# Sixteen key pairs chosen among 80 sums instead of 256, and 80 blocks of activations ahead of the gates in layer 2

## The chip, the cores and the metric

The kernel runs on one core of one Trainium2 chip. The time is device microseconds (us) for one launch, the median of several runs. Beside the runs there is one execution under the hardware profiler; its span and its rows are what the text reads.

## What is computed

Two layers of a hybrid backbone over 256 context tokens and 256 latent tokens with 1024 features. Each layer has a token mixer (attention, a gated delta rule, a linear recurrence) and then a retrieval layer over 16,384 one-neuron experts. The change touches the retrieval layer alone:

```
q = rmsnorm((h @ wq).reshape(ntok, 8, 2, 128))              # 8 heads, 2 halves
s = einsum('nhcd,hckd->nhck', q, subkeys)                   # 128 keys in each half
s_top, i_top = top_k(s, 16)                                 # the 16 best keys of each half
cand = s_top[..., 0, :, None] + s_top[..., 1, None, :]      # 16 x 16 sums of pairs
best, pos = top_k(cand, 16)                                 # the 16 best pairs
idx  = (i_top[..., 0, :, None] * 128 + i_top[..., 1, None, :]) at pos
gate = softmax(best)
act  = gelu(h . u[idx]) * gate;   out = sum over heads and picks of act * v[idx]
```

Layer 1 does this for 512 tokens, layer 2 (the last) for the 256 latent ones only. Since both lists of 16 are sorted, pair (a, b) can be among the 16 best only if (a+1)(b+1) is at most 16.

## The kernel before

**Dense experts.** The kernel doesn't gather rows for most tokens. It computes gelu(h . u) for all 16,384 experts, in 128 blocks of 128 experts, multiplies by a dense gate matrix that is zero where an expert isn't chosen, and multiplies by v. Tokens are columns: N is 384 in layer 1 (the other 128 tokens get their rows by indirect DMA, `fetch`, one row per step on POOL and VectorE) and 256 in layer 2. Each block of u or v (512 KB) is loaded by the SP queue into `wraw` or `vraw` (3 buffers each) and split into a high and a low part: a cast on ScalarE (`wh`, `vh`, L94) and a subtraction on VectorE (`wl`, `vl`, L97). A block of activations is then 8 times three matmuls of N columns (L101 to L103, tile `mm`) and a Gelu on ScalarE (L1006, tile `ge`, 4 buffers).

**Routing.** `queries` computes the scores and the top 16 of each half (`top16`: MAX, MAX_INDEX, MATCH_REPLACE, MAX, MAX_INDEX). `route` then runs `select(g)` for a group of 128 tokens: sums of pairs and `top16` for each of 8 heads, softmax, and for each half a gather of the key's number by comparison with 0..15 (`oh`, `ix`: L1112, L1114, L1116). Layer 1 has four such groups, layer 2 two. After it a loop over passes of 4 tokens builds the gate matrix: VectorE and ScalarE make one-hot rows (`oa`, `ob`), TensorE multiplies them (L1147), ScalarE copies the result to `st` (L1149), and after 32 tokens `st` goes to HBM (2 MB, `gate<-st`). The groups not yet selected are worked off inside this loop.

**Early blocks.** Into both stages `early` puts blocks of activations ahead of the gates: their `ge` is stored to HBM by a DMA on POOL. `REARLY` says how many there are in each layer. One goes with each step of the selects ahead of the loop (20 steps in layer 1, 10 in layer 2), one with every second pass in layer 1 and with every pass in layer 2, and what is left comes after the loop. `experts` afterwards takes the 128 blocks in the order of a list that spreads the late ones (activations not yet computed) among the early ones (activations loaded back, `ge<-early`), multiplies by the gates (`pgt`, loaded for four blocks at a time, L1169 and L1182), splits (`pah`, `pal`) and runs 12 matmuls of 512 columns a block in layer 2.

**What sets the order.** Each engine and the SP queue execute their instructions in one fixed order. A scheduler that builds the program chooses it, from readiness and costs of its own, so that work from different code lines mixes, and an edit changes the order far around it.

Of the kernel before, what the change touches and what calls it, by code (L numbers as in the profile page):

```python
# [13 lines left out]
F32 = mybir.dt.float32  # L14
F32R = mybir.dt.float32r
BF16 = mybir.dt.bfloat16
I32 = mybir.dt.int32
U32 = mybir.dt.uint32
AF = mybir.ActivationFunctionType
ALU = mybir.AluOpType  # L20
# [3 lines left out]
P = 128  # L24
# [15 lines left out]
class Net:  # L40
# [932 lines left out]
    def peer(self, l, T0, x):  # L973
# [3 lines left out]
        gd = self.tc.dram_tile([N // self.TS, P, P, self.TS], F32, name=self.nm("gate"))  # L977
        hd = self.tc.dram_tile([self.REARLY[l], P, N], F32, name=self.nm("early"))
        with self.tc.tile_pool(name=self.nm("gel"), bufs=1, reuse_waits="tile") as gl:
# [16 lines left out]
                next(rows, None)  # L996
            self.rowsdone += 1

    REARLY = (80, 64)
    TS = 32  # L1000

    def expert_h(self, gl, l, j, T0, N):
# [6 lines left out]
    def early(self, gl, l, T0, N, hd, n):  # L1009

        self.wshare = 0.0
        for j in range(self.jearly, min(self.REARLY[l], self.jearly + n)):
            self.nc.gpsimd.dma_start(hd[j], self.expert_h(gl, l, j, T0, N))  # L1013
# [61 lines left out]
    def route(self, rp, l, T0, N, gd, gl, hd, ga, rows, tv, ti, rsN):  # L1075
        nc, V, S, T, I = self.nc, self.V, self.S, self.T, self.I
        mk = lambda shape, tag, dt=F32, bufs=1: self.t(rp, shape, dt, tag, bufs)
        idt, iota = self.C["ident"], self.C["iota"]
        A = NTOK - T0
        NG = A // P  # L1080
        self.jearly = 0
        iT = mk([P, 3, N], "iT")

        def select(g):

            V.tensor_tensor(tv[:, g], tv[:, g], rsN[:, g].unsqueeze(2).to_broadcast([P, 16, 16]), ALU.mult)
            bv, bi = mk([P, 8, 16], "bv"), mk([P, 8, 16], "bi", U32)
            for h in range(8):
                cand, cw = mk([P, 16, 16], "cand", F32, 2), mk([P, 256], "cw", F32, 2)
                V.tensor_tensor(cand, tv[:, g, 2 * h].unsqueeze(2).to_broadcast([P, 16, 16]),  # L1090
                                tv[:, g, 2 * h + 1:2 * h + 2].to_broadcast([P, 16, 16]), ALU.add)
                self.top16(bv[:, h], bi[:, h], cand.rearrange("p a b -> p (a b)"), cw)
                yield
            fetch = g * P >= N
            gt, gs = (ga[1].rearrange("p (a b) -> p a b", b=16) if fetch else mk([P, 8, 16], "gt")), mk([P, 8], "gs")
            V.tensor_tensor(gt, bv, bv[:, :, 0:1].to_broadcast([P, 8, 16]), ALU.subtract)
            S.activation(gt, gt, AF.Exp)
            V.tensor_reduce(gs, gt, AX.X, ALU.add)
            V.reciprocal(gs, gs)
            V.tensor_tensor(gt, gt, gs.unsqueeze(2).to_broadcast([P, 8, 16]), ALU.mult)  # L1100
            tf = mk([P, 16, 16], "tf", BF16)
            V.tensor_copy(tf, ti[:, g])
            sel = []
            for w in range(2):
                pi, pf = mk([P, 8, 16], "pi", U32), mk([P, 8, 16], "pf", BF16)
                if w == 0:
                    V.tensor_scalar(pi, bi, 4, None, ALU.logical_shift_right)
                else:
                    V.tensor_scalar(pi, bi, 15, None, ALU.bitwise_and)
                V.tensor_copy(pf, pi)  # L1110
                oh = mk([P, 8, 16, 16], "oh", BF16, 2)
                V.tensor_tensor(oh.rearrange("p h k v -> p (h k) v"), pf.rearrange("p a b -> p (a b)").unsqueeze(2).to_broadcast([P, P, 16]),  # L1112
                                self.iota16[:, None, :].to_broadcast([P, P, 16]), ALU.is_equal)
                V.tensor_tensor(oh, oh, tf[:, w::2].unsqueeze(2).to_broadcast([P, 8, 16, 16]), ALU.mult)  # L1114
                ix = mk([P, P], "ix", F32, 2)
                V.tensor_reduce(ix, oh.rearrange("p h k v -> p (h k) v"), AX.X, ALU.add)  # L1116
                sel.append(ix)
                yield
            if fetch:
                V.scalar_tensor_tensor(sel[0], sel[1], float(P), sel[0], ALU.mult, ALU.add)  # L1120
                V.tensor_copy(ga[0], sel[0])
                return
            pt = self.px().rearrange("p (a b) -> p a b", a=4)
            for k, src in enumerate((sel[0], sel[1], gt.rearrange("p a b -> p (a b)"))):
                T.transpose(pt[:, k], src, idt)
            S.activation(iT[:, 0, g * P:(g + 1) * P], pt[:, 0], AF.Copy, scale=-1.0)
            S.copy(iT[:, 1:, g * P:(g + 1) * P], pt[:, 1:3])

        for g in ((NG - 1, 0) if ga else (0,)):
            for _ in select(g):  # L1130
                self.early(gl, l, T0, N, hd, 1)
        for n in range(0, N, 4):
            if n % P == 0:
                nxt = select(n // P + 1) if n + P < N else iter(())
            if n % self.TS == 0:
                st = mk([P, P, self.TS], "st", F32, 2)
            pg = (self.px, self.pg, self.acc)[n // 4 % 3]().rearrange("p (a b) -> p a b", a=4)
            a4 = mk([P, 4, P], "oa", F32, 4)
            for k in range(self.OV):
                V.tensor_scalar(a4[:, k], iota, iT[:, 0, n + k:n + k + 1], 0.0, ALU.add, ALU.is_equal)  # L1140
            for k in range(self.OV, 4):
                S.activation(a4[:, k], iota, AF.Abs, bias=iT[:, 0, n + k:n + k + 1])
            S.activation(a4[:, self.OV:], a4[:, self.OV:], AF.Relu, bias=1.0, scale=-1.0)
            for k in range(4):
                b = mk([P, P], "ob", F32, 8)
                ob = V.tensor_scalar(b, iota, iT[:, 1, n + k:n + k + 1], iT[:, 2, n + k:n + k + 1], ALU.is_equal, ALU.mult)  # L1146
                T.matmul(pg[:, k], a4[:, k], b, start=True, stop=True)  # L1147
            m = n % self.TS
            S.copy(st[:, :, m:m + 4].rearrange("p j n -> p n j"), pg)  # L1149
            if m + 4 == self.TS:  # L1150
                nc.scalar.dma_start(gd[n // self.TS], st)
            if n % P % 8 == 0:
                next(nxt, None)
            if n % P == P - 4:
                for _ in nxt:
                    pass
            if n % (self.EV // 2 if T0 else self.EV) == 0:
                self.early(gl, l, T0, N, hd, 1)
            if n % 8:
                self.paced(rows, ob, 1)  # L1160
        self.early(gl, l, T0, N, hd, self.REARLY[l])

# [9 lines left out]
    def expert_terms(self, vp, gl, l, j, T0, N, hd, gt):  # L1172

        nc, I = self.nc, self.I
        mk = lambda shape, tag, dt=F32, bufs=1: self.t(vp, shape, dt, tag, bufs)
        if j < self.REARLY[l]:
            e = self.t(gl, [P, N], F32, "ge", 4)
# [44 lines left out]
    def experts(self, vp, gl, l, T0, N, gd, hd, x, rows):  # L1222

        nc, V, S, T = self.nc, self.V, self.S, self.T
        mk = lambda shape, tag, dt=F32, bufs=1: self.t(vp, shape, dt, tag, bufs)
        E, NT = self.REARLY[l], N // P
        late = [range(j, j + 4) for j in range(E, P, 4)]
# [190 lines left out]
```

## Time and profile before

| | |
|---|---|
| median of 3 runs | 4592.52 us (4588.74 to 4601.06) |
| profiled execution, its own time | 4597.26 us |
| its span | 4595.6 us |
| TensorE busy | 4304.1 us, 94% |
| VectorE busy | 3262.6 us, 71% |
| ScalarE busy | 2345.6 us, 51% |
| granted TensorE clock, mean | 0.96 of full speed |

TensorE is busy nearly all the time, but that is a mean over stages with different limits, and a busy TensorE isn't one at its peak: matmuls overlap, and their ends are modelled. The retrieval layer's routing runs from about 1457 to 1903 us in layer 1 and from 3750 to 4058 us in layer 2; the layer 2 experts follow to 4580 us.

### The profile page before, as it was taken

What the parts mean: (1) busy time and instruction counts of PE and PEld (TensorE: products, weight loads), DVE (VectorE), ACT (ScalarE), POOL (GpSimd) and SP (SyncE); (2) the same over time, 40 slices, a digit from 0 to 9 for tenths busy, and PEclk for the clock granted to TensorE, in tenths of its full rate; (3) what the DMA queues carried; (4) which work ended last, traced back from release to release, by engine and by line L of the source; (5) the groups of instructions that cost most, each with busy time, mean ns of one, the idle gap of its engine ahead of it and who ended that gap; (6) DMA issues with size and microseconds to landing.
All of it is one profiled execution on the core that took longest, in us unless ns stands there. A gap on an engine that the chain in (4) does not pass through costs nothing.

```text
span 4595.6 us, 66921 instructions
## 1 busy us (share of the span) xinstructions
PE 4304.1 (94%) x24379; PEld 3623.5 (79%) x24379; DVE 3262.6 (71%) x7406; ACT 2345.6 (51%) x4145; POOL 453.6 (10%) x428
## 2 busy tenths in 40 slices
PE   6999999999889989999999989989998789989999
PEld 3686877787667889988888856878777689978888
DVE  4767576764469998677888767777675599656665
ACT  4455555553244578533333355656554347844444
POOL 0000000000000222343344300000000001100000
PEclk8999999999999999999999989999998899989999
DMA  4313232225532677899999734223222635676765
GB/s 150 117 60 108 70 106 78 90 72 184 195 106 90 228 253 270 315 335 341 334 334 333 267 119 140 81 83 103 65 83 87 224 131 204 235 238 229 240 231 175
DMA packets 361530, 816.48 MB, mean 178 GB/s; under 512 B 66672, under 2 KB 184944, under 8 KB 357872
## 3 DMA queue, kind: packets, MB, share of 16 engines
q1 hardware_dynamic: 313264, 611.90, 40.3%
q0 software_dynamic: 45056, 158.36, 9.5%
q10 hardware_dynamic: 2880, 41.94, 2.3%
q8 instruction: 191, 3.13, 0.3%
q14 instruction: 139, 1.14, 0.1%
HBM read 713.52 MB, written 98.57 MB: 177 GB/s over the span
## 4 chain that ended last, share of the span: by engine, by line
PE 79%; DVE 11%; DMA 4%; ACT 4%; issue 1%; SPq 0%; ACTq 0%; DVEq 0%
PE mm L103 11%; PE mm L101 11%; PE mm L102 11%; PE acx L101 4%; PE acx L102 4%; PE acx L103 4%; PE px L101 3%; PE px L102 3%; PE px L103 3%; DVE wl L97 2%; DVE ob L1146 1%; PE acg L101 1%; PE acg L103 1%; PE px L872 1%; PE acg L102 1%; DMA wraw<-in_wada 1%
## 5 line engine op out<-in xcount | busy, mean ns | idle before, releaser
L101 PE MATMUL mm<-hh,wh 128*128 128x256 f32 (+2 forms) x2784 | 919.9, 330 | 59.2 <-ACT ge L1006 26.7
L103 PE MATMUL mm<-hh,wl 128*128 128x256 f32 (+2 forms) x2784 | 913.1, 328 | 27.5 <-DVE wl L97 27.1
L102 PE MATMUL mm<-hl,wh 128*128 128x256 f32 (+2 forms) x2784 | 907.7, 326 | 0.0
L94 ACT CAST wh<-wraw 128x1024 fp32r<-128x1024 f32 (+2 forms) x473 | 487.8, 1033 | 697.3 <-PE mm L102 557.2
L97 DVE TENSOR_TENSOR wl<-wraw,wh 128x1024 fp32r<-128x1024 f32 (+2 forms) x473 | 566.2, 1198 | 236.9 <-ACT wh L94 234.8
L101 PEld LDWEIGHTS mm<-hh,wh 128*128 128x128 f32 x2784 | 536.8, 193 | 91.7 <-ACT ge L1006 29.5
L103 PEld LDWEIGHTS mm<-hh,wl 128*128 128x128 f32 x2784 | 535.9, 193 | 59.1 <-DVE wl L97 39.8
L102 PEld LDWEIGHTS mm<-hl,wh 128*128 128x128 f32 x2784 | 536.8, 193 | 23.7 <-issue 2.5
L97 DVE TENSOR_TENSOR vl<-vraw,vh 128x1024 fp32r<-128x1024 f32 x256 | 312.7, 1222 | 148.9 <-ACT vh L94 146.3
L94 ACT CAST vh<-vraw 128x1024 fp32r<-128x1024 f32 x256 | 268.9, 1051 | 280.1 <-PE pg L103 162.6
L94 ACT CAST pah<-ge 128x384 fp32r<-128x384 f32 (+1 forms) x256 | 114.8, 459 | 230.1 <-DVE ge L1182 187.9
L1146 DVE TENSOR_SCALAR ob<-cst,iT 128x128 f32<-128x128 f32 x640 | 183.0, 345 | 55.3 <-PE pg L1147 22.5
L1204 POOL DMA_INDIRECT grow<-in_v,gix x128 | 186.2, 1455 | 252.7 <-DVE gacc L1219 225.8
L1013 POOL DMA_DIRECT2D early<-ge x144 | 80.3, 557 | 1311.7 <-ACT ge L1006 930.9
L101 PE MATMUL mm<-hh,whx 128*128 128x512 f32 (+1 forms) x544 | 203.6, 374 | 2.9 <-ACT tx L800 1.8
L103 PE MATMUL mm<-hh,wlx 128*128 128x512 f32 (+1 forms) x544 | 201.5, 370 | 2.1 <-DVE wlx L97 2.1
L102 PE MATMUL mm<-hl,whx 128*128 128x512 f32 (+1 forms) x544 | 201.8, 371 | 0.0
L101 PE MATMUL px<-vh,pah 128*128 128x512 f32 x512 | 199.5, 390 | 0.0
L102 PE MATMUL px<-vl,pah 128*128 128x512 f32 x512 | 199.3, 389 | 0.0
L103 PE MATMUL px<-vh,pal 128*128 128x512 f32 x512 | 199.1, 389 | 0.0
L1204 POOL DMA_INDIRECT grow<-in_ur,gix x128 | 160.4, 1253 | 303.2 <-DVE gdot L1210 217.5
L1219 DVE SCALAR_TENSOR_TENSOR gacc<-grow,gdot,gacc 128x1024 f32<-128x1024 f32 x127 | 163.1, 1284 | 1.5
(509 smaller groups left out, 10083.3 us busy)
## 6 DMA issues: line engine op xcount, KB each, us to landing
wraw<-in_u SPq DMA_DIRECT2D x256, 512.0 KB
vraw<-in_v SPq DMA_DIRECT2D x256, 512.0 KB
wraw<-in_win SPq DMA_DIRECT2D x192, 512.0 KB
wraw<-in_wada SPq DMA_DIRECT2D x96, 512.0 KB
gate<-st ACTq DMA_DIRECT2D x20, 2048.0 KB
wraw<-in_wbr SPq DMA_DIRECT2D x48, 512.0 KB
pgt<-gate SPq DMA_DIRECT2D x32, 768.0 KB
wraw<-in_wq SPq DMA_DIRECT2D x32, 512.0 KB
```

Of the source, the lines that this page charges most:

```text
L94: self.S.copy(h, src)
L97: return self.V.tensor_tensor(l, src, h.bitcast(F32), ALU.subtract)
L101: mm(out, lh, rh, start=first, stop=False)
L102: mm(out, lh, rl, start=False, stop=False)
L103: mm(out, ll, rh, start=False, stop=last)
L872: T.matmul(sc, a[s, q0:q0 + P], b[s, :nk], start=t == 0, stop=t == 2)
L1013: self.nc.gpsimd.dma_start(hd[j], self.expert_h(gl, l, j, T0, N))
L1146: ob = V.tensor_scalar(b, iota, iT[:, 1, n + k:n + k + 1], iT[:, 2, n + k:n + k + 1], ALU.is_equal, ALU.mult)
L1204: nc.gpsimd.indirect_dma_start(r, None, table, bass.IndirectOffsetOnAxis(ap=ix[:, k:k + 1], axis=0))
L1219: V.scalar_tensor_tensor(acc, r, dot[:, k:k + 1], acc, ALU.mult, ALU.add)
```

## The change

The 256 sums of a head are replaced by 80: a = 0 with all 16 b, a = 1 to 7 with b = 0 to 7, and a = 8 to 15 with b = 0. They are made for all 8 heads at once, by three additions. The search runs over 80 columns. Six small operations on 128 columns turn a place among the 80 into the pair (a, b). And `REARLY` of layer 2 goes from 64 to 80, which layer 1 had already.

```diff
-    REARLY = (80, 64)
+    REARLY = (80, 80)
...
             bv, bi = mk([P, 8, 16], "bv"), mk([P, 8, 16], "bi", U32)
+            cand = mk([P, 8, 80], "cand")
+            s1, s2 = tv[:, g, 0::2], tv[:, g, 1::2]
+            V.tensor_tensor(cand[:, :, :16], s1[:, :, 0:1].to_broadcast([P, 8, 16]), s2, ALU.add)
+            V.tensor_tensor(cand[:, :, 16:72].rearrange("p h (a b) -> p h a b", b=8), s1[:, :, 1:8].unsqueeze(3).to_broadcast([P, 8, 7, 8]),
+                            s2[:, :, :8].unsqueeze(2).to_broadcast([P, 8, 7, 8]), ALU.add)
+            V.tensor_tensor(cand[:, :, 72:], s1[:, :, 8:], s2[:, :, 0:1].to_broadcast([P, 8, 8]), ALU.add)
             for h in range(8):
-                cand, cw = mk([P, 16, 16], "cand", F32, 2), mk([P, 256], "cw", F32, 2)
-                V.tensor_tensor(cand, tv[:, g, 2 * h].unsqueeze(2).to_broadcast([P, 16, 16]),
-                                tv[:, g, 2 * h + 1:2 * h + 2].to_broadcast([P, 16, 16]), ALU.add)
-                self.top16(bv[:, h], bi[:, h], cand.rearrange("p a b -> p (a b)"), cw)
+                self.top16(bv[:, h], bi[:, h], cand[:, h], mk([P, 80], "cw", F32, 2))
                 yield
...
-            for w in range(2):
-                pi, pf = mk([P, 8, 16], "pi", U32), mk([P, 8, 16], "pf", BF16)
-                if w == 0:
-                    V.tensor_scalar(pi, bi, 4, None, ALU.logical_shift_right)
-                else:
-                    V.tensor_scalar(pi, bi, 15, None, ALU.bitwise_and)
-                V.tensor_copy(pf, pi)
+            c8 = lambda tag, dt=BF16: mk([P, 8, 16], tag, dt)
+            hi, lo = c8("phi"), c8("plo")
+            for dst, op, n in ((hi, ALU.logical_shift_right, 3), (lo, ALU.bitwise_and, 7)):
+                pi = mk([P, 8, 16], "pi", U32, 2)
+                V.tensor_scalar(pi, bi, n, None, op)
+                V.tensor_copy(dst, pi)
+            pa, pb, t = c8("pa"), c8("pb"), c8("pt")
+            V.scalar_tensor_tensor(t, hi, 9.0, lo, ALU.is_equal, ALU.mult)
+            V.tensor_scalar(pa, hi, -1.0, 0.0, ALU.add, ALU.max)
+            V.tensor_tensor(pa, pa, t, ALU.add)
+            V.tensor_tensor(lo, lo, t, ALU.subtract)
+            V.tensor_scalar(pb, hi, 1.0, 8.0, ALU.is_equal, ALU.mult)
+            V.tensor_tensor(pb, pb, lo, ALU.add)
+            for w, pf in enumerate((pa, pb)):
```

Three places show how the change moves instructions. The first is VectorE at the start of layer 2's select, right after the scores have been scaled (`tv`); `cand` holds the sums, `bv` and `bi` the chosen values and places, `cw` the working copy. Before:

```order
L1086 TENSOR_TENSOR tv_32942<-tv_32942,rny_33887 128x256 x2
L1090 TENSOR_TENSOR cand_33908<-tv_32942 128x256
L1090 TENSOR_TENSOR cand_33950<-tv_32942 128x256
L1019 MAX bv_33906<-cand_33908 128x8
L1019 MAX bv_33906<-cand_33950 128x8
L1020 MAX_INDEX bi_33907<-bv_33906,cand_33908 128x8
L1021 MATCH_REPLACE cw_33909<-bv_33906,cand_33908 128x256
```

The same place in the changed kernel:

```order
L1090 TENSOR_TENSOR tv_32930<-tv_32930,rny_33875 128x256 x2
L1094 TENSOR_TENSOR cand_33896<-tv_32930 128x8x16
L1095 TENSOR_TENSOR cand_33896<-tv_32930 128x8x56
L1097 TENSOR_TENSOR cand_33896<-tv_32930 128x8x8
L97 TENSOR_TENSOR wl_34070<-wraw_34067,wh_34069 128x1024
L1019 MAX bv_33894<-cand_33896 128x8 x2
L1020 MAX_INDEX bi_33895<-bv_33894,cand_33896 128x8
L1021 MATCH_REPLACE cw_33900<-bv_33894,cand_33896 128x80
```

Three additions stand where each head had one, the searches read 80 columns a head, and a split of a block of u (`wl`) now stands ahead of the first search.

The second place is TensorE at the end of layer 2's gate loop: L1147 (before) and L1161 (changed) are the gate matmuls, `mm` a block of activations, `pah` the experts' own product. Before:

```order
L1147 MATMUL px_37556<-ob_37569,oa_37557 128x128
L1147 MATMUL px_37556<-ob_37572,oa_37557 128x128
L101 MATMUL mm_37790<-hh_32886,wh_37793 128x256
L102 MATMUL mm_37790<-hl_32887,wh_37793 128x256
L103 MATMUL mm_37790<-hh_32886,wl_37794 128x256
L101 MATMUL mm_37790<-hh_32886,wh_37793 128x256
L101 MATMUL acg_37582<-vh_37597,pah_37591 128x512
```

And in the changed kernel, where the block that begins here is followed by six whole blocks and nine matmuls of another before the first `pah`:

```order
L1161 MATMUL px_37844<-ob_37857,oa_37845 128x128
L1161 MATMUL px_37844<-ob_37860,oa_37845 128x128
L101 MATMUL mm_37865<-hh_32874,wh_37868 128x256
L102 MATMUL mm_37865<-hl_32875,wh_37868 128x256
L103 MATMUL mm_37865<-hh_32874,wl_37869 128x256
L101 MATMUL mm_37865<-hh_32874,wh_37868 128x256
```

Four matmuls of a block stood between the last gate matmul and the experts before; now it is 177. The third place is the SP queue around the first load of gates in layer 2. Before, the loads of u and of the first four stored blocks stand ahead of it:

```order
L1178 DMA ge_37651<-early_32930 128x256
L121 DMA wraw_38007<-in_u 128x1024
L121 DMA wraw_38063<-in_u 128x1024
L121 DMA wraw_38119<-in_u 128x1024
L1169 DMA pgt_37586<-gate_32929 128x8x128
L1186 DMA vraw_37595<-in_v 128x1024
```

In the changed kernel two early blocks' loads of u, and all loads of stored blocks, stand behind it:

```order
L121 DMA wraw_38002<-in_u 128x1024
L1183 DMA pgt_38112<-gate_32917 128x8x128
L121 DMA wraw_38036<-in_u 128x1024
L121 DMA wraw_38070<-in_u 128x1024
L1200 DMA vraw_38121<-in_v 128x1024
L1200 DMA vraw_38134<-in_v 128x1024
L1200 DMA vraw_38159<-in_v 128x1024
L1183 DMA pgt_38202<-gate_32917 128x8x128
L1200 DMA vraw_38184<-in_v 128x1024
L121 DMA wraw_38205<-in_u 128x1024
L1200 DMA vraw_38242<-in_v 128x1024
L1192 DMA ge_38114<-early_32918 128x256
```

Of the 80 loads of u for early blocks, 78 are now ahead of the first load of gates and two behind it.

## Rows read from the trace of the kernel before

**Rows 1.** Busy time by stage: window, its length, each engine's busy us (instructions), clock, DMA.

```profile
1457.00:1549.00 92.00, 84.12 (x467) 81.69 (x466) 90.18 (x229) 36.67 (x55) 16.62 (x25) 0.96 0.52 184
1549.00:1741.00 192.00, 171.33 (x1060) 162.65 (x1061) 191.58 (x560) 143.43 (x278) 42.52 (x53) 0.96 0.69 235
1741.00:1869.00 128.00, 126.91 (x850) 126.33 (x850) 110.14 (x312) 107.22 (x206) 35.12 (x43) 1.00 0.85 292
1869.00:1903.00 34.00, 32.11 (x176) 31.38 (x175) 17.43 (x18) 14.96 (x21) 7.97 (x10) 0.95 0.96 353
3750.00:3793.00 43.00, 29.68 (x191) 27.78 (x190) 42.49 (x111) 14.24 (x22) 4.90 (x9) 0.80 0.36 124
3793.00:3868.00 75.00, 70.29 (x561) 68.11 (x561) 73.80 (x212) 60.75 (x115) 9.29 (x17) 0.98 0.60 207
3868.00:4014.00 146.00, 140.64 (x1165) 138.77 (x1165) 99.39 (x261) 118.68 (x227) 19.43 (x36) 0.99 0.64 224
4014.00:4035.00 21.00, 17.53 (x132) 15.88 (x130) 12.65 (x46) 15.80 (x31) 0.54 (x1) 0.95 0.50 183
4035.00:4058.00 23.00, 5.41 (x17) 4.37 (x18) 9.03 (x15) 6.70 (x12) 0.00 (x0) 0.52 0.79 279
4090.00:4580.00 490.00, 490.00 (x2807) 429.74 (x2806) 294.38 (x403) 236.61 (x347) 0.00 (x0) 1.00 0.68 225
```

**Rows 2.** Timeline, TensorE in layer 1's loop, two passes apart: start, length, instruction.

```profile
1802.47 1.05 PE L1147 MATMUL pg<-ob,oa 128*128 128x128 f32 x8
...
1808.42 1.05 PE L1147 MATMUL px<-ob,oa 128*128 128x128 f32 x8
```

**Rows 3.** Timeline, TensorE in layer 2's loop, one pass apart.

```profile
3990.02 1.05 PE L1147 MATMUL px<-ob,oa 128*128 128x128 f32 x8
...
3993.78 1.05 PE L1147 MATMUL pg<-ob,oa 128*128 128x128 f32 x8
3994.67 1.06 PE L1147 MATMUL acx<-ob,oa 128*128 128x128 f32 x8
```

**Rows 4.** Waits, 3750 to 3793: engine, line, waited for: us, times, longest.

```profile
PE mm L103 <- DVE wl L97: 9.7, 3, 7.6
```

**Rows 5.** Waits of TensorE, 1549 to 1741.

```profile
PE mm L103 <- DVE wl L97: 7.0, 10, 1.5
```

**Rows 6.** Timeline of VectorE, 3745 to 3787: searches over 128 and 256 columns, a cast.

```profile
3745.06 0.27 DVE L1022 MAX8 tv<-tw 128x8 f32<-128x128 f32 x1
3745.25 0.07 DVE L1021 MATCH_VALUE_LOAD tw<-tv,sc 128x8 f32 x1
...
3755.34 0.41 DVE L1022 MAX8 bv<-cw 128x8 f32<-128x256 f32 x1
3755.67 0.07 DVE L1021 MATCH_VALUE_LOAD cw<-bv,cand 128x8 f32 x1
...
3785.22 0.22 DVE L1110 CAST pf<-pi 128x128 bf16<-128x128 uint32 x1
```

**Rows 7.** The chain that ended last, 4033 to 4060: start, us, what.

```profile
4033.74 1.24 PE px L1147 x4
4036.09 9.44 DMA gate<-st
4046.02 4.98 DMA vraw<-in_v
4052.59 0.58 PE mm L101
...
4054.75 0.43 PE px L101
...
4059.75 0.23 PE px L102
```

**Rows 8.** Waits of the SP queue, 4000 to 4060.

```profile
SPq L1169 <- DMA gate<-st: 6.9, 1, 6.9
```

**Rows 9.** The chain that ended last, 1884 to 1893, in layer 1.

```profile
1884.07 8.84 DMA vraw<-in_v
```

## The prediction

> **What bounds the kernel now.** I read the busy time by stage first, then the timeline for the price of a pass, then the waits, and last the chain around the end of layer 2's gate loop. In the stages the reader is to see which engine is full [rows 1]. Layer 1's routing has VectorE busy 90.18 of 92 us before the gate loop and 191.58 of 192 us in its first part; there TensorE is busy 171.33 us, at a granted clock of 0.96. From 1741 us on it is the other way round: TensorE 126.91 of 128. Layer 2 repeats this in small: VectorE 42.49 of 43 us before the loop, with TensorE at 29.68 and a clock of 0.80, and 73.80 of 75 while the second select is worked off. From 3868 us TensorE is nearly full, and in the experts entirely (490 of 490). Between them, from 4035 to 4058, TensorE is busy 5.41 of 23 us.
>
> The waits say what TensorE lacks where VectorE is full: the low part of a block of u, which stands in VectorE's queue behind searches. One such wait in layer 2's first select is 7.6 us long [rows 4]; in layer 1's loop ten add up to 7.0 us [rows 5].
>
> The hole at 4035 is the way of the gates through HBM. The last gate matmul ends at 4034.98, the last 2 MB are written from 4036.09 for 9.44 us, a first load behind it lands 4.98 us after 4046.02, and TensorE goes on at 4052.59 [rows 7]. The SP queue waits 6.9 us in this for the write [rows 8]. After it the 512-column matmuls run 0.43 us apart, later 0.23 [rows 7]: the lower of the two clock levels, after TensorE had stood idle.
>
> **The searches.** One search over 128 columns takes 0.19 us of VectorE from start to start, one over 256 columns 0.33, and the load ahead of a replacement 0.06 to 0.07 [rows 6]. That is 0.0011 us a column, so 80 columns cost 0.14. A head had one addition and five searches over 256 columns and three loads: 6 x 0.33 + 0.2 = 2.18 us. It now has five searches over 80: 5 x 0.14 + 0.2 = 0.90. Eight heads save 10.2 us. The three additions cover 128, 448 and 64 columns a partition: 0.19 + 0.54 + 0.12 = 0.85 us. The six new small operations are priced by the 128-column cast, whose length is 0.22 us [rows 6]: 1.3. The shifts and casts of places stay, and so do the gathers. A select saves 8 us. The lower bound takes each search to wait for the end of the one before it: 128 columns last 0.27 us [rows 6], 80 then 0.22, a head costs 1.3, and a select saves 4.9. The order speaks for the upper end: it interleaves two heads, as before.
>
> There are six selects, 48 us of VectorE; the question is how much of it TensorE can use. In layer 1 a block and two passes take 5.95 us when TensorE is the limit [rows 2], so the loop's 48 such pairs need 286 us of the 320 between 1549 and 1869: 34 us of slack. A pass alone takes 0.89, a layer 2 pass with its block 3.76 [rows 3], so a block costs 2.87 us in layer 2 and 5.95 - 1.78 = 4.17 in layer 1. Ahead of the loop 20 blocks need 83 of 92 us. Four selects free 32 us of VectorE against 43 of slack. I take 24 of 32: the gathers remain as bursts in which a pass must wait for VectorE whatever the searches cost. Bounds are 12, where the shorter prices meet those bursts, and 32.
>
> Layer 2's first select is wholly VectorE's: 8 us (5 to 9), as its ten blocks need 28.7 of 43. In the second, 561 matmuls are 17.5 passes with a block, 66 of 75 us [rows 1, 3]: I take 5 of the 8 freed (2 to 8). The selects together give 37 us (19 to 49).
>
> **The 16 blocks.** They leave the experts, where TensorE is full, so 16 x 2.87 = 46 us go from there [rows 1, 3]. They come back on TensorE earlier; the gain is what they find idle. Ten go into the last ten passes. Those took 21 us, from 4014 to 4035, in which 132 matmuls ran: 80 of passes and 52 of blocks that the scheduler had drawn ahead, 8.9 + 6.2 = 15.1 us of need, so 6 us lost. In the stage before, 1165 matmuls are 36.4 passes with a block, 137 us of 146: 0.25 lost a pass [rows 1, 3]. Ten such passes lose 2.5. Gain 3.
>
> In the hole 7.4 blocks now follow the last pass, 21 us of work. The idle time was 17.6 us (4052.59 - 4034.98), and some 12 matmuls at 0.43 in place of 0.23 made it 2.5 longer [rows 7]: 20. Not all goes away. Two of the loads of u stand behind the load of gates in SP's order, and that waits for the write, which lands 10.5 us after the last pass. Five blocks cover 14.4 us. The sixth's load, by the nearest row some 5 us [rows 7], lands at 15.5, and the cast ahead of its first matmul makes it 16.5 to 17: 2.5 us idle. The stored blocks' loads stand behind five loads of v, of which the fourth waits for a free buffer, that is for the first one's cast and subtraction. I put them out at 19.5 and their landing, multiplication and split at 25, when the blocks have ended near 23: 2 more. The clock falls in such pauses: another 2.5. So 7 us stay, and 13 are gained. Edits with one answer: the stores and loads of 16 x 128 KB are hidden by TensorE's work, at a DMA share of 0.68 in the experts [rows 1]; without that cover they are 4 MB, or 19 us at that stage's 225 GB/s. Gain of this part 16 us, with bounds 3 and 23.
>
> The Trainium skill (Trainium Kernel Development and Optimization, Key Constraints) says that transfers issued from SP, ACT and POOL share the same 16 DMA engines and interleave. By it the early blocks' loads lengthen the gate write; six of them are 3.1 MB, and if all of that ran ahead of the chain at the 279 GB/s of that stage, the hole would keep 11 us more and this part would give 5 in place of 16.
>
> Against that stands layer 1, which already has blocks in this place: from 1869 to 1903 TensorE is busy 32.11 of 34 us at a clock of 0.95, with the DMA engines at 0.96 [rows 1], though one load there takes 8.84 us [rows 9]. I keep 16.
>
> **Sum.** 37 + 16 = 53 us off the profiled execution's 4597.3: 4544. That execution is 4.7 us above the median shown, so 4540.
>
> **The rivals.** First, *the hole stays*: loads bunch up behind the gates, each as slow as layer 1's 8.84 us [rows 9]. The sixth block then starts near 23, the stored blocks are ready near 37, and the idle time is 16 us with some 4 of low clock: all that was there. Only the 3 us of the passes remain, 40 in all: 4552. For it speaks the order on SP, against it layer 1's full TensorE.
>
> Second, *the searches save less*: chained searches at 0.22 us, and passes that wait for gathers. The selects give 19, in all 35: 4557. For it speaks that only part of layer 1's idle time lies at the searches. Third, *all is used*: 49 + 23 us: 4520. VectorE's full stages speak for it, the bursts against. Fourth, *both fail*, the searches giving 10 us and the blocks 3: 4579.
>
> The other side: *slower, by the SP queue*. The load of gates waits for the write, and two loads of u and everything later wait behind it. Five blocks cover 14.4 us from the last pass; each us that the write lands later is then a us of idle TensorE. It landed after 10.5 us. To use up 53 us it would have to land some 60 us after the last pass; at 75 it gives 4607. Nothing in the rows comes near: the chain's longest transfer is 9.44 us.
>
> **How the numbers follow.** Forecast 0.55, the hole stays 0.15, searches save less 0.15, all is used 0.09, both fail 0.04, slower 0.02. The low end of the range is the upper bounds' sum of 72 us, 4520, a little widened; the high end the lower bounds, 19 + 3 = 22 us, 4570. No change within measurement is 0.3%, 14 us. Only both failing together comes there, so faster has 0.94.
>
> **What would show it.** Searches over 80 columns 0.14 us apart, and VectorE's busy time about 48 us lower; the loop of layer 1 near 300 us instead of 320; layer 2's stretch before the loop near 35 instead of 43; an idle TensorE of about 5 us, not 17.6, behind the last pass; the experts 46 us shorter. Wrong it would be if layer 1's loop kept its length, since TensorE's waits would then not have been the searches', or if the hole only moved behind the sixth block.

## The result, and the profile of the changed kernel

The changed kernel takes 4542.93 us (median of 4 runs, 4536.66 to 4545.33), the kernel before beside it 4596.39 (4 runs, 4588.74 to 4601.06). The ratio is 0.9883, with a 95% interval of 0.9864 to 0.9902: 53 us less, where 4540 us and a sum of 53 were forecast. The total hides errors in its terms: the searches gave more than forecast, the 16 blocks less.

The profiled execution took 4536.66 us, its span is 4535.0. The page's line of busy times:

```profile
PE 4283.0 (94%) x24379; PEld 3612.7 (80%) x24379; DVE 3214.4 (71%) x7412; ACT 2348.0 (52%) x4145; POOL 457.7 (10%) x444
```

VectorE is 48.2 us less busy than before (3262.6), which is the forecast's figure. The busy time by stage of the changed kernel (the columns of [rows 1]):

```profile
1441.00:1533.00 92.00, 87.33 (x503) 84.52 (x501) 91.63 (x322) 39.59 (x59) 17.63 (x26) 1.00 0.54 185
1533.00:1830.00 297.00, 288.35 (x1911) 285.42 (x1911) 273.77 (x809) 251.00 (x483) 77.66 (x95) 1.00 0.81 278
1533.00:1600.00 67.00, 62.43 (x408) 60.65 (x409) 65.67 (x212) 56.84 (x111) 17.07 (x21) 1.00 0.77 256
1600.00:1650.00 50.00, 46.08 (x301) 45.12 (x300) 49.93 (x162) 40.83 (x79) 12.84 (x16) 1.00 0.78 263
...
3707.00:3748.00 41.00, 34.21 (x249) 31.59 (x250) 40.17 (x136) 19.62 (x34) 5.54 (x10) 0.96 0.46 145
3748.00:3830.00 82.00, 77.91 (x628) 75.81 (x627) 75.22 (x241) 66.54 (x129) 9.86 (x18) 0.98 0.61 205
...
4002.00:4034.00 32.00, 24.55 (x182) 22.81 (x182) 14.22 (x14) 14.87 (x22) 4.34 (x8) 0.95 0.87 309
4034.00:4526.00 492.00, 491.49 (x2678) 425.07 (x2678) 299.78 (x425) 237.73 (x346) 0.00 (x0) 1.00 0.72 234
```

Layer 1's gate loop lasts 297 us instead of 320, and VectorE is full only in its first 117 us, before in the first 192. Layer 2's first select is still VectorE's (40.17 of 41). From the end of the scores to the first gate matmul it lasts 41.1 us; before it was 51.8, of which the window of [rows 1] leaves out the first 7. The whole of it before:

```profile
3743.00:3795.00 52.00, 37.84 (x252) 35.38 (x252) 50.82 (x146) 20.76 (x37) 5.50 (x10) 0.83 0.36 119
```

VectorE does 10.65 us less work in this stretch and the stretch is 10.7 us shorter; TensorE's clock in it rose from 0.83 to 0.96. Between the last pass and the experts 177 matmuls run where there were 4. The experts last 492 us instead of 534, 42 us less and not the 46 of the forecast: 341 matmuls have left them, 14.2 blocks and not 16, since parts of two had been drawn ahead of them before.

VectorE's timeline in that select: searches start 0.15 us apart and the load ahead of one takes 0.05 to 0.06 (0.14 and 0.06 to 0.07 were forecast; [rows 6] has 0.33 for 256 columns):

```profile
3720.10 0.23 DVE L1022 MAX8 bv<-cw 128x8 f32<-128x80 f32 x1
3720.25 0.07 DVE L1021 MATCH_VALUE_LOAD cw<-bv,cand 128x8 f32 x1
3720.30 0.23 DVE L1021 MATCH_REPLACE8 cw<-bv,cand 128x80 f32<-128x80 f32 x1
3720.45 0.08 DVE L1023 MATCH_VALUE_LOAD bi<-bv,cw 128x8 f32 x1
```

Of TensorE's waits in layer 1's loop, those for the low part of u fell to 2.1 us in three waits (before, from 1549 to 1741 alone, [rows 5]):

```profile
PE mm L103 <- DVE wl L97: 2.1, 3, 1.1
```

The table holds, for each stretch, what TensorE lost in it: its length (between the matmuls that bound it) less its matmuls at the steps that the traces show at full clock (0.11 us for 128 columns, 0.12 for 256, 0.17 for 384, 0.23 for 512; rounded here, and the third place moves a row by some 7 us at most, but the differences between these four kernels by less than 0.5). The last two kernels are the first two experiments below.

| lost, us | before | changed | searches alone | blocks alone |
|---|---|---|---|---|
| layer 1, select and loop | 51.4 | 22.4 | 23.7 | 51.5 |
| layer 2, first select | 22.4 | 11.8 | 11.8 | 22.3 |
| layer 2, loop | 24.5 | 18.7 | 21.1 | 20.1 |
| last pass to first `pah` (the hole) | 18.5 | 10.8 | 18.2 | 10.4 |
| experts of layer 2 | 8.2 | 7.2 | 7.8 | 9.9 |
| sum | 125.0 | 70.9 | 82.6 | 114.2 |

The sums differ from before by 54.1, 42.4 and 10.8 us; the medians by 53, 39 and 9.

The chain around the hole, which answers to [rows 7]:

```profile
4004.04 8.69 DMA gate<-st
4012.75 0.38 SPq L1183
...
4014.61 7.52 DMA vraw<-in_v
...
4023.24 1.24 DVE vl L97
4024.49 3.47 DMA vraw<-in_v
...
4030.31 1.05 ACT wh L94
...
4031.38 1.24 DVE wl L97
...
4034.53 0.43 PE acg L101
```

The last gate matmul ends at 4002.64. The gates can be loaded 10.1 us later (4012.75), a first load of v lands 7.52 us after its issue, and a fourth goes out only at 4024.49, when the first one's buffer is free. The first product of the experts comes 32 us behind the last pass. Behind the early blocks TensorE pauses 3.15 us (4028.25 to 4031.40, from start to start), until `wh` of the block that follows is ready; six shorter pauses of 0.48 to 1.68 us lie ahead of it, one of 0.88 behind. The `pah` matmuls begin 0.43 us apart again, eight of them.

The first two of these pauses, 1.68 us at 4008 and 0.72 at 4010, don't come from the loads. TensorE waits there for two casts (`wh`) whose loads had landed at 4000.09 and 4003.84 by the DMA semaphores in the trace. The casts stand behind the second block's Gelu in ScalarE's order:

```profile
4008.43 0.39 ACT L1006 ACTIVATE ge<-mm 128x256 f32<-128x256 f32 x1 [2.49 <-PE mm L103]
4008.71 1.98 ACT L94 CAST wh<-wraw 128x1024 fp32r<-128x1024 f32 x2
```

Every kernel here with 80 or more blocks in layer 2 has both pauses; they are 2.2 of the 10.8 us in the table.

SP's waits around the hole, which answer to [rows 8]:

```profile
SPq L1200 <- DVE vl L97: 11.5, 4, 6.0
SPq L1183 <- DMA gate<-st: 8.4, 1, 8.4
```

### The profile page after: what moved, and what is told of

Read it like the earlier page. It is cut to its first block, busy times and chain, and to the rows that moved or that the text cites. A ratio compares the mean times of both kernels' runs of the same rounds, so it can differ in the third digit from the quotient of the medians.

```text
span 4535.0 us, 67054 instructions
## 1 busy us (share of the span) xinstructions
PE 4283.0 (94%) x24379; PEld 3612.7 (80%) x24379; DVE 3214.4 (71%) x7412; ACT 2348.0 (52%) x4145; POOL 457.7 (10%) x444
## 4 chain that ended last, share of the span: by engine, by line
PE 81%; DVE 10%; ACT 4%; DMA 4%; issue 1%; SPq 0%; ACTq 0%; DVEq 0%
PE mm L103 11%; PE mm L101 11%; PE mm L102 11%; PE acx L101 4%; PE acx L102 4%; PE acx L103 4%; PE px L101 3%; PE px L102 3%; PE px L103 3%; DVE wl L97 2%; PE acg L103 1%; PE acg L101 1%; PE px L872 1%; PE acg L102 1%; PE pg L102 1%; PE pg L101 1%
```

## The experiments

Each time is a median beside the kernel before on the same chip. Three questions were open. Do the two parts add up, and which term is off? What share of the freed VectorE time does TensorE use? And what keeps the hole from closing? For the last one the theories were SP's waits (the gates' write, later the loads of v), casts of v in the way on ScalarE, and the DMA engines themselves.

**The searches alone.** The changed kernel with 64 early blocks:

```diff
-    REARLY = (80, 80)
+    REARLY = (80, 64)
```

> The 80 sums alone, with 64 blocks ahead in layer 2 as before. Theory A (the searches free VectorE where TensorE waits for it): about 40 us less than before, near 4556, ratio 0.991, with layer 1's gate loop near 297 us from its first to its last matmul and layer 2's stretch between the scores and the loop near 41. Theory B (most of the gain comes with the 16 blocks and the new order, not with the searches): at most the 11 us of layer 2's first select, near 4585.

Measured: 4555.25 us (4547.22 to 4557.23), ratio 0.9913 (0.9900 to 0.9927): 39 us less than before, where the forecast's terms add to 37 and theory A had 4556. The table shows 27.7 in layer 1, 10.6 in the first select of layer 2 and 3.4 in its loop.

**The blocks alone.** The kernel before with 80 early blocks:

```diff
-    REARLY = (80, 64)
+    REARLY = (80, 80)
```

> The 16 blocks alone, with 256 sums as before. Theory A: about 12 us less than before, near 4584, ratio 0.997, since the last ten passes and the hole behind them are filled in the same way. Theory B: 40 us or more less. Theory C (the hole only moves behind the sixth block and the scheduler's two late blocks did the rest already): within 3 us of before.

Measured: 4585.48 (4576.52 to 4590.49), 0.9979 (0.9970 to 0.9988), 9 us less; theory A had 4584. The two parts add up: 39 + 9 = 48 by medians and 42.4 + 10.8 = 53.2 by the table, against 53 and 54.1 for both. The term of the blocks is the one that was too large.

**Gates loaded through POOL.** If the remaining hole is SP waiting for the gates' write, with loads of u and v behind it, a load that waits on POOL sets them free:

```diff
-        self.nc.sync.dma_start(gt, gd[:, :, j:j + 4].rearrange("c i j n -> i c j n"))
+        (self.nc.gpsimd if self.T0 else self.nc.sync).dma_start(gt, gd[:, :, j:j + 4].rearrange("c i j n -> i c j n"))
```

> The changed kernel with layer 2's loads of gates issued by POOL instead of SP. Theory A (what is left of the hole is SP standing 8.4 us at the first load of gates, with two loads of u and all of v behind it): the 11 us that TensorE still loses there fall to 3 or 4, near 4536, and the sixth block no longer waits. Theory D (the loads share the DMA engines, and these are the limit there): no change, near 4543.

Measured: 4547.20 (4542.62 to 4554.84), 0.9903 (0.9888 to 0.9918): no gain. The hole is 33.0 us long, the experts lose 11.3. The chain of this run shows why:

```profile
4010.49 9.77 DMA vraw<-in_v
...
4022.62 9.92 DMA vraw<-in_v
```

A load of v now goes out 0.3 us behind the write of the gates instead of 10.6, and takes 9.77 us instead of 7.52; the next one takes 9.92. Much of what SP waited for before is now waited for in the transfers. The gain of theory A is not there. The edit did not set SP free, though: the two loads of u go out at 4017.15 and 4018.29, because SP now waits for `wl`, that is for a free buffer. What SP's wait is worth is left to the five buffers below.

**72, 96 and 112 blocks.** The changed kernel with `REARLY` of layer 2 at 72, 96 and 112.

> The changed kernel with 72 blocks ahead in layer 2: eight more than before, all of them inside the passes, none behind the last one. Theory A (the passes give 4 us, the blocks behind the last pass the rest): the hole loses 18 us again, and the three stretches from the loop to the end of the experts are 785 us long (792.7 before, 788.5 with the searches alone, 778.2 changed), in all near 4551. Theory F (it is the count of stored blocks that helps, wherever they run): half of the gain, near 4548, with the hole half as long.

> The changed kernel with 96 blocks ahead in layer 2. Theory A: 22 blocks, 63 us of TensorE, stand behind the last pass, longer than the 32 us until the first product of the experts, so only the wait of the sixth block, some 4 us, stays of the 11: near 4537. Theory D: more stores and loads in the same stretch cost what they cover, 4543 or more.

> The changed kernel with 112 blocks ahead in layer 2. Theory A: as with 96, since the chain behind the last pass is covered already: 4535 to 4538, the three stretches within 3 us of the 770.4 of 96. Theory D (stores and loads cost DMA time): more than 3 us longer than with 96.

The stretches are those of layer 2 from the first gate matmul to the experts' end, by length; the 64 are the searches alone.

| early blocks | median, us | ratio (interval) | stretches, us | hole and experts, lost |
|---|---|---|---|---|
| 64 | 4555.25 | 0.9913 (0.9900 to 0.9927) | 788.5 | 18.2 + 7.8 |
| 72 | 4550.18 | 0.9896 (0.9881 to 0.9912) | 782.2 | 11.9 + 9.5 |
| 80 | 4542.93 | 0.9883 (0.9864 to 0.9902) | 778.2 | 10.8 + 7.2 |
| 96 | 4536.43 | 0.9872 (0.9857 to 0.9887) | 770.4 | 7.8 + 3.9 |
| 112 | 4539.87 | 0.9878 (0.9863 to 0.9894) | 769.0 | 9.2 + 1.1 |

The rows come from several chips; by the difference from the kernel before on the same chip they are 39, 49, 53, 58 and 60 us less. The 72 don't separate their two theories (4551 and 4548 expected). The stretch of 782.2 us is 3 below what theory A had, and the hole loses 11.9 us and not 18, because the edit did not do what A took it to do: two whole blocks stand behind its last pass, not none. The 112 come out 2 to 5 us above what was expected of them, on a chip where the kernel before took 5 us longer than beside the 96; by the difference they are where they were expected. The first 16 blocks give 10 us of stretch, the next 16 eight (13 and 3 in the series below), the last 16 nothing that can be told from no change. With 96 the work outlasts the loads: the clock stays at 1.00 through the 32 us behind the last pass, in which TensorE is busy 27.98 us (24.55 in the changed kernel). A row of that kernel by window (the last gate matmul is at 4009; run again, see below):

```profile
4009.00:4041.00 32.00, 27.98 (x222) 26.72 (x220) 14.86 (x13) 16.12 (x23) 4.86 (x9) 1.00 0.88 326
```

**Fewer splits of v in the way.** In the chain `wh` of the block that follows stands right behind a cast and a subtraction of v. With two split buffers instead of four in layer 2 the third and fourth cast of v move behind that `wh`:

```diff
-    VB = (4, 4)
+    VB = (4, 2)
```

> The changed kernel with two buffers in place of four for the split blocks of v in layer 2, so that on ScalarE the cast of the first late block of u stands behind two casts of v and not four. Theory E (what is left of the hole is this cast, which waits for v's fourth load): the first product of the experts comes 4 us earlier behind the last pass (28 in place of 32), near 4539, if the experts don't lose by having fewer buffers. Theory D (the rate of the loads): no change there.

Measured: 4555.86 (4546.84 to 4563.22), 0.9908 (0.9895 to 0.9922), 44 us less than before where the changed kernel has 53. The casts were not the cause: the third and fourth no longer stand ahead of `wh`, and its load of u landed at 4029.80, 16.8 us after the load of gates went out, in the changed kernel 17.5. So at most 0.7 us was theirs. `wh` starts 17.56 us after the load of gates in both (4030.53 - 4012.97, in the changed kernel 4030.31 - 4012.75), but that is chance: in this run it stands behind the Gelu of the block before (4030.26), whose matmuls ran 0.21 us apart instead of 0.12.

```profile
4012.97 0.38 SPq L1183
...
4025.79 4.46 issue
...
4030.53 1.04 ACT wh L94
```

What the edit costs lies in the experts, where the stretch grew from 492 to 503 us because TensorE now waits for splits (waits of TensorE from 4034 to 4537):

```profile
PE acg L102 <- DVE vl L97: 7.0, 8, 2.0
```

**Searches over 176 columns.** The sums padded to 176 columns, so that about half of what the searches save is taken back:

```diff
-            cand = mk([P, 8, 80], "cand")
+            cand = mk([P, 8, 176], "cand")
+            V.memset(cand[:, :, 80:], -3.0e38)
...
-                self.top16(bv[:, h], bi[:, h], cand[:, h], mk([P, 80], "cw", F32, 2))
+                self.top16(bv[:, h], bi[:, h], cand[:, h], mk([P, 176], "cw", F32, 2))
```

> The changed kernel with each head's 80 sums padded to 176 columns by a constant that is never chosen: each search costs 0.10 us more, a select 4.0, and one fill of some 0.9. Theory A (VectorE's time in the searches is what TensorE waits for): layer 1's stretch from the scores to the loop's end gets 15 to 20 us longer, layer 2's first select 5, the second 1 or 2: 4563 to 4570. Theory B (it was the new order, not the searches' time): 5 us or less.

Measured: 4565.02 (4559.84 to 4573.78), 0.9933 (0.9919 to 0.9946), 34 us less than before where the changed kernel has 53. Searches start 0.25 us apart:

```profile
3741.48 0.32 DVE L1022 MAX8 bv<-cw 128x8 f32<-128x176 f32 x1
3741.73 0.32 DVE L1019 MAX8 bv<-cand 128x8 f32<-128x176 f32 x1
3741.97 0.07 DVE L1023 MATCH_VALUE_LOAD bi<-bv,cw 128x8 f32 x1
```

This is within what theory A had (4563 to 4570). VectorE's busy time is 3239.8 us, 22.8 below before instead of 48.2: 3.8 us a select instead of 8.0. Layer 1 lost 39.3 us instead of 51.4: 12.1 gained where its four selects freed 15.2, a share of 0.8. In the changed kernel it is 29.0 of 32, 0.9. The forecast had 0.75. Layer 2's first select is 6.3 us longer than in the changed kernel (5 expected), the second not longer (1 or 2 expected). VectorE is full in the first one again (45.23 of 47; the clock is 0.89):

```profile
3727.00:3774.00 47.00, 35.61 (x248) 33.55 (x247) 45.23 (x138) 19.08 (x32) 5.47 (x10) 0.89 0.40 128
```

**Five raw buffers of v; 96 blocks again; both.** In the changed kernel the load of u for the block behind the pause went out at 4024.86, behind the fourth load of v, and landed at 4030.23, just ahead of its `wh` (by the DMA semaphores in the trace). With five raw buffers in layer 2 that load of v waits for nothing; the order on TensorE and ScalarE is the same:

```diff
-        raw = mk([P, 1024], "vraw", F32, 3)
+        raw = mk([P, 1024], "vraw", F32, (3, 5)[l])
...
-            y = mk([P, 1024], "vraw", F32, 3)
+            y = mk([P, 1024], "vraw", F32, (3, 5)[l])
```

It ran together with the changed kernel as it is, the 96 blocks, and 96 blocks with five buffers.

> The changed kernel as it is, beside the three others of this series. It should come out near 4543 us again, 53 us below the kernel before; the three stretches from the scores of layer 2 to the first product behind the last pass and the experts add up to 778 us, as in the first profile of it, and the stretches that no edit touches differ from that profile by up to some 10 us.

> 96 blocks ahead of the gates in layer 2, beside the changed kernel on the same chip. If the 8 us by which its layer 2 stretches were shorter (770.4 against 778.2) are real, its median is 5 to 10 us below that of the changed kernel. If they are scatter, the two medians agree within 3 us.

> The changed kernel with five raw buffers of v in layer 2 instead of three; the order on TensorE and ScalarE stays as it is, and on SP the fourth load of v moves ahead of the load of gates and waits for nothing. Theory G, that the end of the hole is SP's wait: the load of u for the block that begins the experts was issued 22.5 us after the last gate matmul only because the fourth load of v ahead of it waited for the first one's subtraction (11.5 us of waits on SP). Without that wait it goes out 8 us earlier, the pause of 3.15 us ahead of that block is gone, the first product of the experts comes 2 to 4 us earlier, and the stretch from the last pass to it falls from 32 to 28 to 30 us. Theory H, that it is the DMA engines, which are nearly full behind the gates: the same bytes land as late as before, whatever order they go out in, the first product comes within 1 us of where it was, and the time is that of the changed kernel. In the experts themselves, where TensorE is full, both expect nothing.

> Both together: five raw buffers of v and 96 blocks. With 96 blocks there is work left on TensorE long after the loads behind the gates have landed, so neither theory expects the buffers to add anything: the time of the 96 blocks alone, within 3 us. If the two gains added up, it would be 2 to 4 us below it.

| | median, us | runs | ratio (interval) | stretches, us |
|---|---|---|---|---|
| changed, again | 4545.54 | 4542.34 to 4555.79 | 0.9887 (0.9869 to 0.9905) | 775.5 |
| 96 blocks, again | 4538.98 | 4530.08 to 4555.13 | 0.9876 (0.9856 to 0.9896) | 772.7 |
| five buffers | 4542.72 | 4529.92 to 4543.25 | 0.9870 (0.9852 to 0.9888) | 774.7 |
| five buffers and 96 | 4531.11 | 4521.75 to 4543.60 | 0.9852 (0.9831 to 0.9872) | 772.6 |

With five buffers SP's waits for `vl` shrink from 11.5 us to one of 1.0 (waits of SP, 3998 to 4045):

```profile
SPq L1183 <- DMA gate<-st: 9.1, 1, 9.1
...
SPq L1200 <- DVE vl L97: 1.0, 1, 1.0
```

The load of u goes out 4.8 us after the load of gates instead of 12.1, and lands 15.9 us after it instead of 17.5: seven us earlier out, 1.6 earlier in. The hole is 30.4 us long, against 32.0 and 30.9 in the two profiles of the changed kernel. So theory G, SP's wait, is worth at most 1.6 us, and theory H, the DMA engines, holds for the rest but for the 2.2 us of ScalarE's order. The windows of the changed kernel behind the write of the gates show it (the last three columns are the clock, the DMA share and GB/s):

```profile
4013.00:4017.00 4.00, 4.00 (x36) 4.00 (x35) 1.22 (x1) 1.33 (x2) 0.54 (x1) 1.00 0.70 228
4017.00:4030.00 13.00, 9.27 (x69) 8.25 (x67) 6.80 (x6) 7.10 (x10) 2.02 (x4) 1.00 1.01 349
4030.00:4034.00 4.00, 2.13 (x8) 1.84 (x9) 2.61 (x5) 1.78 (x3) 0.15 (x1) 0.62 0.75 254
```

and the same with five buffers:

```profile
4019.00:4031.00 12.00, 9.62 (x64) 9.01 (x62) 6.99 (x6) 7.13 (x11) 1.62 (x3) 0.86 1.04 396
```

The DMA engines are full from the landing of the gates (4016.77) until that load of u is in (4030.23). What they move at that share is not one rate: 349 GB/s here, 396 with five buffers. Nine loads of 512 KB stand in between in either order (two of gates, three of u, four of v).

The 96 blocks are 6.5 and 6.6 us below the changed kernel by the medians of both series (4.3 in the first by the differences from the kernel before), and 5 us by the stretches (771.6 against 776.9, means of two); single runs overlap, so the gain is likely but not shown. The lowest median is that of both edits, 8 us below the 96 blocks, where nothing or 2 to 4 us was expected. But its stretches equal those of the 96 blocks alone, so nothing in the stretches that the buffers touch accounts for the 8 us; whether they are real stays open.

## Why the prediction was right, and where its terms were off

**Searches, layer 1: 24 forecast, 29 measured** (27.7 with the searches alone). The mechanism was right: the searches over 80 columns start 0.15 us apart, VectorE lost 48 us of work, and the waits for `wl` fell. That it was the searches' time and not the new order is shown by the 176 columns, which give back what they cost. The share of the freed time that TensorE would use was set too low, 0.75 in place of 0.9. The bursts of gathers, for which a quarter was set aside, cost little.

**Searches, layer 2: 8 and 5 forecast, 10.6 and 3.4 measured.** In the first select TensorE gained more than the 8.0 us that a select gives. VectorE's rows show why: it is full in that stretch before and after, and its work in it fell by 10.65 us. Before, 72 instructions of the searches stood there, more than the 64 of one select, because a first head of the second select was searched in it; in the changed kernel there are 64. So the new order moved some 2 us of VectorE's work into the second select, where less was then used than forecast. With 176 columns VectorE does 5.6 us less there and 4.3 are gained. TensorE's clock rose as well (0.83 before, 0.89 with 176 columns, 0.96 with 80), but a full VectorE sets the length of the stretch, so no gain is shown to be the clock's. The sum, 14, is near the 13 forecast.

**The blocks in the passes: 3 forecast, 4.4 measured with the blocks alone, 2.4 on top of the searches.** The size is right within what two profiles can tell.

**The hole: 13 forecast, 8.1 measured with the blocks alone, 7.4 on top of the searches.** (With the blocks alone 1.7 were lost again in the experts, in the changed kernel nothing.) This is the term that was mis-sized; the blocks' part is 11 instead of 16. The step that failed is the one in which the stored blocks' loads were put "out at 19.5" and ready "at 25", so that 7 us would stay, where the table has 10.8. The sixth block's load, "by the nearest row some 5 us", was nearly right: it took 5.71 us and landed 16.3 us after the last pass, where 15.5 was forecast. Behind it the loads bunch up, because the early blocks and the experts ask for nine loads, 4.7 MB, within 17.5 us. A first load of v takes 7.52 us, and those behind it land 1.1 to 2.3 us apart. The 4.98 us of [rows 7] was a load with one load of gates ahead of it. The first stored block's load went out 24.6 us after the last pass and landed at 29.5, the load of u for the block that leads the experts landed at 27.6, and the first product came at 31.7. The fourth load of v did wait for a free buffer, as the text said, but an early end of that wait moves the landing by 1.6 us only. The forecast also left out the 2.2 us that ScalarE's order takes behind the second block.

The rival by which the blocks' transfers and the gates' write share the DMA engines had 5 us for this part, the forecast 16; the runs give 9 by medians and 11 by the table, between the two. It did not come in the form in which it was priced: the write of the gates was not lengthened (8.69 us, before 9.44); it was the loads behind it that waited for one another, at a DMA share of 1.01. A stored block of 128 KB from POOL's queue took 2.0 us before the write (3999.52 to 4001.52) and 6.4 us among SP's loads (4015.51 to 4021.95). The Trainium skill (Trainium Kernel Development and Optimization, Key Constraints) says that transfers of the SP, ACT and POOL queues run on the same DMA engines and interleave. These two times agree with it. Layer 1, which was brought against the rule, showed only that TensorE had work enough there; its DMA share of 0.96 [rows 1] was the warning.

**The rivals.** *The hole stays* was nearer the truth than its chance of 0.15 says: its picture of bunched loads is what happened, at less than half its price. *The searches save less* is excluded by the searches alone (39 us, it had 19). *All is used* had 49 us for the searches; they gave 39 by medians and 42 by the table, nearer to the 37 of the forecast, and the blocks stayed far below its 23. *Both fail* is excluded by the same run (it had 10 for the searches). *Slower, by the SP queue* fell at its first term: the write landed 10.1 us after the last pass, before 10.5.

The whole came out at 4543, 3 us from the forecast, because 5 us too little in layer 1 and 5 too much in the hole cancel; that part of the agreement is luck.

## What to carry to other kernels

Where one engine is full in a stage, time taken from it there comes back nearly whole. What the stage gains is read from that engine's busy time in the same stretch, from one event to another, because the new order may move other work into or out of it. When work is put into a gap that a transfer makes, count the bytes that the new work and the next stage ask for in the same gap, and divide by the rate that the trace shows there; a load's time from a row with less ahead of it is too short. Before an edit frees a waiting queue, look at the DMA share behind the wait: here, at 1.0, a transfer that was issued seven us earlier landed 1.6 us earlier.

## What the runs showed of the hardware that was not expected

The searches keep the forecast's line down to 80 columns: 0.15, 0.19, 0.25 and 0.33 us from start to start for 80, 128, 176 and 256 columns, 0.001 us for each further column.

Stretches that no edit here touches differ between executions. From the start to the end of layer 1's scores the fourteen profiles have 1438.1 to 1449.4 us, and from the end of layer 1's experts to the end of layer 2's scores 1093.8 to 1112.3. The spans of two profiles can thus differ by ten us for no reason of the edit (60.6 us between those of before and after, where the medians say 53), and a stretch has to be compared with the same stretch.
